# One list for the z units and gate pairs of an encoder layer, and a later place for gate/up's evictions and down sums

## The chip, the core and the metric

The kernel runs on one core of one Trainium2 chip. The metric is the device time of one execution in microseconds (us). It uses five engines: TensorE (PE, with its weight loads as PEld), VectorE (DVE), ScalarE (ACT), GpSimd (POOL) and SyncE (SP, which here issues the DMAs).

## The reference, cut to what matters

One layer of a bidirectional encoder is computed over 1024 tokens and 16 meta tokens, with a model width of 1024, in float32:

```python
h = rmsnorm(h_res, norm1_w[l])
proj = h @ w_in[l]
(q, k, v, z, b_raw, a_raw, sc_b, sc_c, sc_x, gate_a, gate_b) = jnp.split(proj, SPLIT_POINTS, axis=-1)
o_dn = gated_deltanet_bidir(q, k, v, z, b_raw, a_raw, dn_conv_w[l], A_log[l], dt_bias[l], dn_norm_w[l])
y_a = o_dn @ w_branch_dn[l]
y_b = (sc_b * depthwise_conv_centred(sc_c * sc_x, sc_conv_w[l])) @ w_branch_sc[l]
merged = jax.nn.sigmoid(gate_a) * y_a + jax.nn.sigmoid(gate_b) * y_b
h_res = h_res + merged @ w_out[l]
h2 = rmsnorm(h_res, norm2_w[l])
gu = h2 @ w_gate_up[l]
h_res = h_res + (jax.nn.silu(gu[..., :D_FF]) * gu[..., D_FF:]) @ w_down[l]
```

The change touches two stages: the columns z, gate_a and gate_b of the first projection (in `gated_deltanet_bidir` z is used through silu(z)), and `gu` with silu(gate) * up.

## The kernel before, in words

**Numbers as pairs.** Every float32 operand of a product is split in a high part, which ACT casts (`split`, L101), and a low part, which DVE subtracts (L102, `sub` is L179). A product term then takes three matmuls: weight high by data high, weight high by data low, weight low by data high. The matmuls treated here multiply a 128x128 block of weights with 512 tokens.

**The first stage ("z/pair section").** After the scans of the first half of the heads come four *z units*, heads 4 to 7: for each, 128 columns of w_in are loaded, split, and multiplied with the two token halves (24 matmuls each, `dense`, L134 to L136). ACT takes the tanh of half the bank (L1505), DVE makes z*(1+tanh) of it (L1507), SP stores it (L1508). Then come five *gate pairs*, n = 0 to 4 for column blocks j = 3 to 7: gate A's and gate B's block of 128 columns by the two token halves. A pair is done by a scheme of seven products in place of eight: P1 = A11·B11, P2 = A12·B21, S2·T2, S1·T1, S3·T3, S4·B22 and A22·T4 ("TT"), 12 matmuls each (`product`, L1443). Here S1 to S4 are sums of weight blocks ("b1" to "b4": `sums`, L1417 to L1420, with their splits in `stationary2`), T1 to T4 sums of token blocks (`moving_sums`, each formed by DVE in passes 2048 or 1024 elements wide, its high part cast by ACT in one pass of 2048, L1460, its low part subtracted by DVE). T1 to T4 are formed once and serve all pairs. Partial results share a PSUM bank: S2·T2 is added onto P1 in its bank, S3·T3 onto that. So ACT must have copied the bank out before the next product is added: c1 (L1574, into o1's left half) before S2·T2, c2 (L1584) and c3 (L1586) before S3·T3 and S4·B22. DVE adds the other partial results (L1409), ACT takes tanh (`half_turn`, L1511), SP stores both gates (L1597, L1598).

The order of the section up to pair 1 is the order of the code on DVE, PE and ACT: it stands under a manual schedule (`border0`), in which generators (`z_rows`, `pair`, `moving_sums`) are advanced step by step. Pairs 2 to 4 follow outside it, where a scheduler may move instructions. SP's and POOL's queues are ordered by the scheduler throughout. Tiles come from pools: a new tile in the place of an old one waits until the old one's readers are done. The tile that the first token sums are written to (tag `mA`) lies where the stage before had its own tiles.

**Gate/up.** From about 1367 us, 22 columns j of w_gate_up go through the same seven products, 84 matmuls a column. `part1` does P1 and P2 of a column with the copy of the bank, and, unless postponed, the add and Silu (L1765, L1768). Columns 0, 1 and 2 do their `part1` ahead of the loop; the add and Silu of 1 and 2 (`late_evictions`) are called inside column 0. Within a column: the block weights (`block22`, `sums`, `stationary2`), S2·T2, copy u2 (L1847), S1·T1, copy u3 (L1849), S3·T3, add, S4·B22, add, Silu (L1862), multiply, TT, multiply (L1410), stores of the product to DRAM (L1868, L1869). DVE stands under a manual schedule from before column 0 until `border.close()`. `down_sums(k)` loads two blocks of w_down (L1777, L1778), forms four sums on DVE (`sums<-sums`, L179) and stores them (t_d, L1781); it is called for k = j-3 in column j. The sums are read in the last stage only.

Of the kernel before, what the change touches and what calls it, by code (L numbers as in the profile page):

```python
# [8 lines left out]
F32 = mybir.dt.float32  # L9
# [7 lines left out]
P = 128  # L17
# [31 lines left out]
def encoder_layer(ctx: ExitStack, tc: tile.TileContext, x, meta, norm1_w, w_in, w_ba,  # L49
# [1395 lines left out]
    def moving_sums():  # L1445
# [14 lines left out]
        high = lambda n, t: nc.scalar.copy(mov[n][0], t)  # L1460
# [30 lines left out]
        yield
# [5 lines left out]
    z_units = [wload(w_in, unit(OZ + ZH * P))]  # L1497

    def z_rows(h):

        sz = s4(SEQ)
        for sl in (left, right):
            po = psz()
            dense(po, z_units[h - ZH], hx, C0 + META + sl.start, 512)
            nc.scalar.activation(sz[:, sl], po, AF.Tanh, scale=0.5)  # L1505
            yield
            nc.vector.scalar_tensor_tensor(out=sz[:, sl], in0=sz[:, sl], scalar=1.0, in1=po, op0=ALU.add, op1=ALU.mult)  # L1507
        nc.sync.dma_start(z_d[h], sz)  # L1508
        yield
# [3 lines left out]
    def pair_weights(n, j):  # L1513

        s_hl[n % 2] = big(("mB", "mA")[n % 2], [P, 2, 2, KT, P])
        if n == 0:
# [20 lines left out]
        return A_, first, block_sums, second

    def pair(n, j, A_, first, block_sums, second):

        last = j == KT - 1
        o1, o2 = outs[n] = s4(), s4()
        bank = pss()
        if last:
# [474 lines left out]
```

## Time and profile before

| what | value |
|---|---|
| median of the runs shown | 2000.35 us (2000.34, 2000.35, 2001.31) |
| the profiled execution's own time | 2001.08 us |
| its span (first to last instruction) | 1999.33 us, so 1.75 us lie around it |
| granted TensorE clock, mean | 0.998 |
| PE busy | 1972.3 us, 11999 matmuls |
| DVE, ACT, POOL busy | 1396.7, 838.6, 107.0 us |
| z/pair section | 934.95 to 1064 us |
| gate/up, columns 0 to 10 | 1367 to 1580 us |

In the rows of the trace the first number is the start in us, the second the length, then engine, line, operation, the tile written and the tiles read, shapes, a count (several instructions of a kind in a row are one line), and in brackets how long the engine had been idle and what released it. In the rows by stretches the columns are: stretch and its length, busy time and count of PE, PEld, DVE, ACT and POOL, the granted PE clock, the busy share of the DMA engines, GB/s.

### The profile page before, as it was taken

To read this page: it belongs to the slowest core of one execution; us is meant where nothing else is said; L and a number is where in the kernel's file an instruction comes from. 1 tells how busy PE (TensorE), PEld (TensorE's weight loads), DVE (VectorE), ACT (ScalarE), POOL (GpSimd) and SP (SyncE) were. 2 spreads that over 40 slices of the span, in tenths; PEclk is the share of its full clock that TensorE was granted. 3 is DMA by queue.
4 is the path that set the end of the run, shared out by engine and by line. 5 is a ranking of instruction groups with operands and counts; after the bars stand their busy time and mean duration, and the time that the engine had idled before them with its cause. 6 is when DMAs were issued, how large, how long until landed. Compare 5 with 4: busy or idle time off the path is not lost.

```text
span 1999.3 us, 31850 instructions
## 1 busy us (share of the span) xinstructions
PE 1972.3 (99%) x11999; PEld 1718.4 (86%) x11999; DVE 1396.7 (70%) x3015; ACT 838.6 (42%) x1967; POOL 107.0 (5%) x407
## 2 busy tenths in 40 slices
PE   9999999999999999999899999999999999999998
PEld 8999999999999999888778888887878888888887
DVE  6888688888888888846845544468766666656575
ACT  6472354646464646343334221225333333334344
POOL 2011101010101010100000000000000000000000
PEclk9999999999999999999999999999999999999999
DMA  3122222222122212223236743123665345487654
GB/s 133 66 90 74 59 86 59 75 59 75 59 75 59 86 58 65 74 82 104 84 123 236 253 156 96 64 88 124 246 218 209 135 149 188 158 274 243 194 169 173
DMA packets 124546, 251.00 MB, mean 126 GB/s; under 512 B 44966, under 2 KB 46423, under 8 KB 121960
## 3 DMA queue, kind: packets, MB, share of 16 engines
q1 hardware_dynamic: 123815, 247.92, 37.3%
q8 instruction: 94, 1.54, 0.3%
q10 hardware_dynamic: 576, 1.05, 0.1%
q14 instruction: 61, 0.49, 0.1%
HBM read 180.67 MB, written 68.25 MB: 125 GB/s over the span
## 4 chain that ended last, share of the span: by engine, by line
PE 84%; DVE 8%; DMA 4%; ACT 3%; issue 1%; SPq 0%; DVEq 0%; ACTq 0%
PE pm L341 31%; PE pd L1443 10%; PE pe L1443 4%; PE pm L1443 3%; DMA sums<-in_w_down_dram 2%; PE pd L903 1%; PE pd L882 1%; PE pd L866 1%; PE pd L869 1%; PE pe L1927 1%; PE pe L1925 1%; PE pe L1926 1%; PE pd L899 1%; PE pe L603 1%; PE pd L1927 1%
## 5 line engine op out<-in xcount | busy, mean ns | idle before, releaser
L341 PE MATMUL pm<-hTh,wh 128*128 128x320 f32 (+4 forms) x1248 | 428.0, 348 | 0.4 <-ACT hTh L1103 0.2
L341 PE MATMUL pm<-al,wh 128*128 128x320 f32 (+4 forms) x1248 | 427.3, 348 | 0.0
L341 PE MATMUL pm<-hTh,wl 128*128 128x320 f32 (+4 forms) x1248 | 425.6, 346 | 0.0
L341 PEld LDWEIGHTS pm<-hTh,wh 128*128 128x128 f32 x1248 | 233.7, 188 | 12.0 <-issue 1.3
L341 PEld LDWEIGHTS pm<-hTh,wl 128*128 128x128 f32 x1248 | 234.0, 188 | 10.2 <-issue 0.4
L341 PEld LDWEIGHTS pm<-al,wh 128*128 128x128 f32 x1248 | 233.9, 188 | 9.7
L102 DVE TENSOR_TENSOR al<-raw,ring_h 128x1024 fp32r<-128x1024 f32 x73 | 88.6, 1222 | 64.9 <-ACT ring_h L101 64.1
L101 ACT CAST ring_h<-raw 128x1024 fp32r<-128x1024 f32 x73 | 76.7, 1054 | 106.9 <-PE pe L1927 35.0
L363 DVE SCALAR_TENSOR_TENSOR kq<-ra,wc,kq 128x520 f32<-128x520 f32 x128 | 96.5, 754 | 4.9 <-ACT kq L393 4.0
L990 DVE TENSOR_TENSOR wl<-raw,wh 128x512 fp32r<-128x512 f32 x112 | 75.9, 688 | 31.0 <-ACT wh L993 30.4
L889 ACT ACTIVATE w<-pd,small 128x128 f32<-128x128 f32 x128 | 39.8, 363 | 125.0 <-PE pd L882 124.5
L101 ACT CAST wh<-raw 128x1024 fp32r<-128x1024 f32 x49 | 51.4, 1048 | 70.6 <-PE pm L135 17.7
L500 DVE TENSOR_TENSOR fP<-fP,tm 128x135 f32<-128x135 f32 (+23 forms) x248 | 71.7, 289 | 5.1
L496 DVE TENSOR_TENSOR tm<-fP,fN 128x135 f32<-128x135 f32 (+23 forms) x248 | 71.5, 289 | 4.4
L102 DVE TENSOR_TENSOR wl<-raw,wh 128x1024 fp32r<-128x1024 f32 x49 | 59.7, 1219 | 19.4 <-ACT wh L101 19.3
L993 ACT CAST wh<-raw 128x512 fp32r<-128x512 f32 x112 | 66.2, 621 | 3.7 <-issue 3.6
L1862 ACT ACTIVATE b<-b 128x512 f32<-128x512 f32 x22 | 13.9, 631 | 116.2 <-DVE b L1409 116.2
L1409 DVE TENSOR_TENSOR b<-pd,b 128x512 f32<-128x512 f32 x22 | 15.2, 690 | 64.4 <-PE pd L1443 64.4
L1443 PE MATMUL pd<-b,mB 128*128 128x512 f32 x204 | 52.0, 403 | 5.7 <-ACT s L1574 4.9
L1443 PE MATMUL pd<-b_hl,wh 128*128 128x512 f32 x176 | 54.4, 390 | 0.0
L1443 PEld LDWEIGHTS pd<-b,mB 128*128 128x128 f32 x204 | 39.5, 195 | 15.5 <-ACT s L1574 5.3
L856 ACT ACTIVATE jk<-NP 128x128 f32<-128x128 f32 x64 | 19.9, 311 | 76.4 <-DVE NP L852 75.4
(589 smaller groups left out, 4741.9 us busy)
## 6 DMA issues: line engine op xcount, KB each, us to landing
raw<-in_w_in_dram SPq DMA_DIRECT2D x72, 512.0 KB
raw<-in_w_gate_up_dram SPq DMA_DIRECT2D x44, 512.0 KB
sums<-in_w_down_dram SPq DMA_DIRECT2D x22, 512.0 KB
t_d<-sums SPq DMA_DIRECT2D x11, 1024.0 KB
raw<-s_d SPq DMA_DIRECT2D x44, 256.0 KB
raw<-t_d SPq DMA_DIRECT2D x44, 256.0 KB
act_d<-b SPq DMA_DIRECT2D x43, 256.0 KB
raw<-act_d SPq DMA_DIRECT2D x33, 256.0 KB
```

The lines of the kernel that those rows point to most:

```text
L101: nc.scalar.copy(hi, src)
L102: nc.vector.tensor_tensor(out=lo, in0=src, in1=hi.bitcast(F32), op=ALU.subtract)
L341: mm(po[:, :n], ww[:, k], f(k)[:, t0:t0 + n], start=i == 0, stop=i == 3 * KT - 1)
L363: nc.vector.scalar_tensor_tensor(out=acc, in0=raw[:, h0 + t:h0 + t + hn], scalar=wc[:, t, col:col + 1], in1=acc, op0=ALU.mult, op1=ALU.add)
L496: nc.vector.tensor_tensor(out=tv, in0=fP[:, 0:r, j:j + 1].broadcast_to([P, r, n]), in1=fN[:, j:j + 1, j + 1:32].broadcast_to([P, r, n]), o ...
L500: nc.vector.tensor_tensor(out=fP[:, 0:r, j + 1:32], in0=fP[:, 0:r, j + 1:32], in1=tv, op=ALU.subtract)
L603: mm(pk[:, :2 * P].rearrange("p (a t) -> p a t", a=2), kT[:, cs(c)], kq[:, :, cs(c)], start=True, stop=True)
L889: nc.scalar.activation(w[d], b2[:, 2 + d], AF.Copy, scale=ce[:, c, d:d + 1])
L990: nc.vector.tensor_tensor(out=u[1][1][:, k], in0=u[2][:, k], in1=u[1][0][:, k].bitcast(F32), op=ALU.subtract)
L993: nc.scalar.copy(u[1][0][:, k], u[2][:, k])
L1443: mm(po, x[:, k], at(y, k), start=i == 0 and not add_to, stop=i == 11, skip_group_check=add_to)
L1927: mm(bank[t], l_[:, c], h_[:, hi], start=False, stop=last)
```

## The change

In the z/pair section the generators go. Every step (a load's split, a product, a copy, a sum) gets a name, and one list, `SECTION`, names the order in which they are called: T1a to T4c are the passes of the token sums, T1h and T1l a high and low part, z5.0 the products of head 5's first half with its tanh (z5.0t) and finish (z5.0s), g0h, u0h, b01 to b04, sa0h to sb0l the weights of pair 0, P1_0 to TT_0 its products, c, a and h its copies, adds and tanhs. Pairs 2 and 3 follow in the order `PAIR`, S3·T3 now before S4·B22 in all of them. The casts that were L1460, L101 are L1467, L1529, L1538 and L1546 now, the copies c1 to c3 are L1559, tanh L1503 and L1516, the gates' loads L1522 and L1523.

```diff
         f = lambda m: m.bitcast(F32)
@@ -1457,191 +1459,193 @@
         x, y = (big(g, [P, 2, 4, 512], F32) for g in ("mA", "b3"))
         t1, t2, t3, d_ = x[:, 0], x[:, 1], y[:, 0], y[:, 1]
...
-        high = lambda n, t: nc.scalar.copy(mov[n][0], t)
-        low_part = lambda n, t: sub(mov[n][1], t, f(mov[n][0]))
-        sub(t1, h0[1], h0[0])
-        sub(d_, l0[1], l0[0])
-        add(t1, t1, d_)
-        high("T1", t1)
-        yield
...
-        high("T4", t1)
-        yield
-        low_part("T4", t1)
-        yield
+
+        def high(n, t):
+            if n == "T4":
+                m = big("b3", [P, 2, 4, 512])
+                mov[n] = m[:, 0], m[:, 1]
+            nc.scalar.copy(mov[n][0], t)
+        steps.update(T1a=lambda: sub(t1, h0[1], h0[0]), T1b=lambda: sub(d_, l0[1], l0[0]), T1c=lambda: add(t1, t1, d_),
...
+            steps[n + "h"] = lambda n=n, t=t: high(n, t)
+            steps[n + "l"] = lambda n=n, t=t: sub(mov[n][1], t, f(mov[n][0]))
```

```diff
-    outs = {}
-    sums_of_blocks = moving_sums()
-    z0, z1, z2, z3 = (z_rows(h) for h in range(ZH, H))
-    z_units.append(wload(w_in, unit(OZ + (ZH + 1) * P)))
-    next(z0)
-    next(sums_of_blocks)
-    next(sums_of_blocks)
-    next(z0)
-    z_units.append(wload(w_in, unit(OZ + (ZH + 2) * P)))
...
-    pair0 = pair(0, GH, *weights0)
-    weights1 = pair_weights(1, GH + 1)
-    next(pair0)
-    weights1[1]()
-    weights1[2]()
-    for _ in pair0:
-        pass
-    pair1 = pair(1, GH + 1, *weights1)
-    for _ in pair1:
-        pass
```

```diff
+        def sum_high(i):
+            if i == 0:
+                a["s"] = big(("mB", "mA")[n % 2], [P, 2, 2, KT, P])
+            sh, sl = (a["s"][:, m, i] for m in range(2))
+            for x, k in enumerate((("S2", "S4"), ("S3", "S1"))[i]):
+                A_[k] = sh[:, 4 * x:4 * x + 4], sl[:, 4 * x:4 * x + 4]
...
+             "sah": lambda: sum_high(0), "sal": lambda: low_of(a["s"][:, 1, 0], rg, a["s"][:, 0, 0]),
+             "sbh": lambda: sum_high(1), "sbl": lambda: low_of(a["s"][:, 1, 1], ru, a["s"][:, 0, 1]),
+             "P1": lambda: into("bank", "A11", "B11"), "c1": lambda: taken("o1", left, "bank"),
+             "P2": lambda: into("p2", "A12", "B21"), "a1": lambda: added("o1", left, "p2"),
+             "h1": lambda: half_turn(a["o1"][:, left]),
+             "S2": lambda: into("bank", "S2", "T2", True), "c2": lambda: taken("o1", right, "bank"),
+             "S1": lambda: into("bank2", "S1", "T1"), "c3": lambda: taken("o2", right, "bank2"),
+             "S3": lambda: into("bank", "S3", "T3", True), "a3": lambda: added("o2", right, "bank"),
+             "h3": lambda: half_turn(a["o2"][:, right]),
+             "S4": lambda: into("bank2", "S4", "B22", True), "a2": lambda: added("o1", right, "bank2"),
+             "h2": lambda: half_turn(a["o1"][:, right]),
+             "TT": lambda: into("bank", "A22", "T4", True), "h4": last_turn}
+        return d, A_, a, rg, ru, out_tile, stores
...
+    SECTION = """
+        T1a z4.0 z5h T1b z5l T1c z4.1 z4.0t T2a T1h z4.0s T2b T2c z5.0 z4.1t T3a z6h u0h T2h z4.1s z6l u0l
+        b01 z5.1 z5.0t b02 z5.0s T3b T3c T2l z6.0 z5.1t z7h z5.1s T3d z7l T3h T1l z6.1 z6.0t z6.0s T4a T3l
+        z7.0 z6.1t g0h z6.1s u1h g0l b03 b04 T4b sa0h z7.1 z7.0t T4c sb0h z7.0s T4h sa0l sb0l T4l P1_0 z7.1t
+        g1h z7.1s g1l P2_0 c1_0 u1l b11 b12 S2_0 a1_0 b13 h1_0 b14 sa1h S1_0 c2_0 sa1l sb1h sb1l S3_0 c3_0
+        S4_0 a3_0 h3_0 TT_0 a2_0 h2_0 P1_1 h4_0 P2_1 c1_1 S2_1 a1_1 h1_1 S1_1 c2_1 S3_1 c3_1 S4_1 a3_1 h3_1
+        TT_1 a2_1 h2_1 h4_1
+    """
...
+    for k in SECTION.split():
+        steps[k]()
     border0.close()
...
+    for n, j in enumerate(range(GH + 2, KT - 1), 2):
+        d = pair_steps(n, j)[0]
+        for k in PAIR.split():
+            d[k]()
```

In gate/up the block weights of column 1 are written within column 0, and those of column 2 within column 1; `late_evictions` moves from before S4·B22 to behind TT of column 0; DVE's manual schedule ends a column later; the down sums are called for k = j-6 in place of j-3.

```diff
@@ -1826,15 +1830,18 @@
     late_evictions = [p[-1] for p in ahead[1:]]
     split(*mov["T3"], m32[3])
     u_hl[0] = big("w2", [P, 2, 4, P])
+
+    def block_weights(j, rg, ru, A_):
+        block22(j, ru, A_)
+        sums(rg, ru, rg[:, 0:4], rg[:, 4:8], ru[:, 0:4], ru[:, 4:8])
+        stationary2(j, ru, rg, ru, A_)
+
     for j in range(NF):
+        rg, ru, A_, p1, sg, bank, _ = ahead.pop(0) if ahead else part1(stationary1(j), sm[:, j % 2], sm[:, 2 + j % 2])
         if j == 1:
-            s_hl[1] = ap_.tile([P, 2, 2, KT, P], F32R, tag="al0", name="s_hl1")
-            u_hl[1] = ap_.tile([P, 2, 4, P], F32R, tag="al2", name="u_hl1")
-        rg, ru, A_, p1, sg, bank, _ = ahead.pop(0) if ahead else part1(stationary1(j), sm[:, j % 2], sm[:, 2 + j % 2])
-        if j:
-            block22(j, ru, A_)
-            sums(rg, ru, rg[:, 0:4], rg[:, 4:8], ru[:, 0:4], ru[:, 4:8])
-            stationary2(j, ru, rg, ru, A_)
+            block_weights(2, *ahead[0][:3])
+        elif j > 2:
+            block_weights(j, rg, ru, A_)
         u2, u3, r2 = sm[:, 4 + j % 2], sm[:, 6], sm[:, 7]
         if j >= HK:
             k = j - HK
@@ -1855,8 +1862,9 @@
         add(u3, bank, u3)
         if j == 0:
             split(*mov["T4"], m32[2])
-            for f in late_evictions:
-                f()
+            s_hl[1] = ap_.tile([P, 2, 2, KT, P], F32R, tag="al0", name="s_hl1")
+            u_hl[1] = ap_.tile([P, 2, 4, P], F32R, tag="al2", name="u_hl1")
+            block_weights(1, *ahead[0][:3])
         product(bank2, A_["S4"], "B22", True)
         add(u2, bank2, u2)
         nc.scalar.activation(u2, u2, AF.Silu)
@@ -1864,11 +1872,14 @@
         product(bank, A_["A22"], "T4", True, lows_last=j == 0)
         mul(sg, bank, sg)
         if j == 0:
+            for f in late_evictions:
+                f()
+        elif j == 1:
             border.close()
         nc.sync.dma_start(act_d[j][:, 0:512], sg)
         nc.sync.dma_start(act_d[j][:, 512:1024], r2)
-        if 3 <= j <= HK + 2:
-            down_sums(j - 3)
+        if 6 <= j <= HK + 5:
+            down_sums(j - 6)
         if j >= HK:
 
             s1, s4_ = p1, u2
```

What this does to the queues is shown at three places. First DVE, at the start of the z/pair section: `rb` is the last tile of the stage before, `mA` and `b` the tiles of the token sums, `wl` a weight's low part; in brackets what an instruction waits for (DMAHW are DMA queues). Before:

```order
L478 SCALAR_TENSOR_TENSOR rb_12122<-rb_12122,pm_12072 128x512 [waits DMAHW5_49,Activation_49]
L179 TENSOR_TENSOR mA_12177<-hTh 128x2048
L179 TENSOR_TENSOR b_2076_12178<-al_124 128x2048
L1409 TENSOR_TENSOR mA_12177<-mA_12177,b_2076_12178 128x2048 [waits DVE_49]
L179 TENSOR_TENSOR mA_12177<-hTh,mA_12177 128x2048 [waits DVE_49]
L1409 TENSOR_TENSOR mA_12177<-mA_12177,al_125 128x1024 [waits DVE_49]
```

And after the change:

```order
L478 SCALAR_TENSOR_TENSOR rb_12122<-rb_12122,pm_12072 128x512 [waits DMAHW5_49,Activation_49]
L179 TENSOR_TENSOR mA_12138<-hTh 128x2048 [waits DMAHW1_49,DMAHW4_49,DMAHW0_49,DVE_49]
L179 TENSOR_TENSOR b_2068_12139<-al_124 128x2048
L179 TENSOR_TENSOR wl_12187<-raw_12142,wh_12186 128x1024 [waits DMAHW6_49,PE_49]
L1409 TENSOR_TENSOR mA_12138<-mA_12138,b_2068_12139 128x2048 [waits DVE_49]
L179 TENSOR_TENSOR mA_12138<-hTh,mA_12138 128x2048 [waits DVE_49]
L1507 SCALAR_TENSOR_TENSOR s_2083_12217<-s_2083_12217,pe_12161 128x512 [waits Activation_49]
```

The first pass on `mA` waits for three DMA queues now, before for none; the low part `wl` and a finish of a z unit stand among the passes.

Second ACT, around the copies of pair 0 (`s<-pd` are c1 and c2, `wh`, `u_hl` and `mB` or `mA` the high parts of weights). Before:

```order
L101 CAST mB_12318<-raw_12323 128x1024
L1460 CAST b_2098_12396<-mA_12177 128x2048
L1505 ACTIVATE s_2096_12359<-pe_12401 128x512
L1574 COPY s_2107_12439<-pd_12441 128x512
L1511 ACTIVATE s_2107_12439<-s_2107_12439 128x512
L101 CAST wh_12433<-raw_12435 128x1024
L101 CAST u_hl_12431<-raw_12436 128x512
L101 CAST wh_12655<-raw_12657 128x1024
L1584 COPY s_2107_12439<-pd_12441 128x512
```

And after the change:

```order
L1467 CAST b_2103_12429<-mA_12138 128x2048
L1503 ACTIVATE s_2102_12424<-pe_12399 128x512
L1529 CAST wh_12448<-raw_12152 128x1024
L1559 COPY s_2108_12467<-pd_12434 128x512
L1529 CAST wh_12658<-raw_12654 128x1024
L1516 ACTIVATE s_2108_12467<-s_2108_12467 128x512
L1546 CAST mA_12488<-raw_12152 128x1024
L1559 COPY s_2108_12467<-pd_12434 128x512
L1546 CAST mA_12488<-raw_12153 128x1024
```

The cast of T4 stands ahead of c1 in both. Pair 1's high part of a block sum (L1546, `mA<-raw`) stands ahead of c2 now, where before two casts of pair 1's plain weights and pair 2's did.

Third DVE in gate/up, from the low part of T4 (`b<-al`, L102) in column 0 on. Before:

```order
L1409 TENSOR_TENSOR b_2363_14871<-pd_14912,b_2363_14871 128x512
L1417 TENSOR_TENSOR raw_14889<-raw_14889 128x512
L1418 TENSOR_TENSOR raw_14889<-raw_14888,raw_14889 128x512
L102 TENSOR_TENSOR b_2384_14993<-al_14128,b_2384_14993 128x2048
L1409 TENSOR_TENSOR b_2363_14871<-pe_14979,b_2363_14871 128x512
L1409 TENSOR_TENSOR t_2391_15004<-pm_15019,t_2390_15003 128x512
L1409 TENSOR_TENSOR b_2363_14871<-pe_15035,b_2363_14871 128x512
L1419 TENSOR_TENSOR raw_14888<-raw_14889,raw_14888 128x512
L102 TENSOR_TENSOR s_hl_15118<-raw_14889,s_hl_15118 128x1024
L1410 TENSOR_TENSOR b_2363_14871<-b_2363_14871 128x512
L1410 TENSOR_TENSOR b_2363_14871<-pd_14912,b_2363_14871 128x512
L1420 TENSOR_TENSOR raw_14888<-raw_14888 128x512
```

And after the change:

```order
L102 TENSOR_TENSOR b_2384_14993<-al_14128,b_2384_14993 128x2048
L102 TENSOR_TENSOR u_hl_15084<-raw_14889,u_hl_15084 128x512
L1417 TENSOR_TENSOR raw_14889<-raw_14889 128x512
L1418 TENSOR_TENSOR raw_14889<-raw_14888,raw_14889 128x512
L1419 TENSOR_TENSOR raw_14888<-raw_14889,raw_14888 128x512
L1420 TENSOR_TENSOR raw_14888<-raw_14888 128x512
L179 TENSOR_TENSOR sums_15748<-sums_15748 128x512
L102 TENSOR_TENSOR s_hl_15083<-raw_14888,s_hl_15083 128x1024
L102 TENSOR_TENSOR s_hl_15083<-raw_14889,s_hl_15083 128x1024
```

Column 1's four block sums and the low part `u_hl` follow T4's low part at once, with one pass of the down sums between; the four adds and two multiplies that stood among them come later.

More of the change, by code (lines that the diff above doesn't have):

```diff
@@ L1443, in product, with moving_steps @@
             mm(po, x[:, k], at(y, k), start=i == 0 and not add_to, stop=i == 11, skip_group_check=add_to)
-    def moving_sums():
+    steps = {}
+    def moving_steps():
         c = [slice(C0 + META + 512 * i, C0 + META + 512 * i + 512) for i in range(2)]
@@ L1644, in encoder_layer, with high, corner @@
-    o1 = outs[KT - 1 - GH][0]
+        g0, g1, u0, u1 = rg[:, 0:4], rg[:, 4:8], ru[:, 0:4], ru[:, 4:8]
+        def high():
+            gh, gl = a["g"] = wtiles([P, KT, P])
+            A_["A11"], A_["A12"] = (gh[:, 0:4], gl[:, 0:4]), (gh[:, 4:8], gl[:, 4:8])
+            nc.scalar.copy(gh, rg)
+        def corner():
+            if n == 0:
+                u = big("w2", [P, 2, 4, P])
+                u_hl[0] = u[:, 0], u[:, 1]
+            elif n == 1:
+                u_hl[1] = [tp.tile([P, 4, P], F32R, tag="t2", name=uid("u_hl"), bufs=2) for _ in range(2)]
+            A_["A22"] = u_hl[n % 2]
+            nc.scalar.copy(u_hl[n % 2][0], u1)
```

232 lines of the change are left out of this document (100 added, 132 removed).

## The prediction

> **What bounds the kernel now.** I read the page's busy times first, then the 40 slices, then stretches where PE falls short, and there the waits and the timeline.
>
> ```profile
> PE 1972.3 (99%) x11999; PEld 1718.4 (86%) x11999; DVE 1396.7 (70%) x3015; ACT 838.6 (42%) x1967; POOL 107.0 (5%) x407
> 950.00:1000.00 50.00, 44.46 (x186) 35.98 (x185) 39.96 (x37) 18.61 (x23) 0.00 (x0) 0.93 0.24 84
> 1350.00:1400.00 50.00, 46.07 (x210) 36.66 (x208) 44.05 (x58) 26.45 (x32) 0.00 (x0) 1.00 0.36 125
> PE pd L1443 <- ACT s L1574: 4.9, 1, 4.9
> ```
>
> PE bounds: all its idle time is 1999.3 − 1972.3 = 27 us, and the change touches no matmul, so it can only win or lose idle time and clock. PE lacks most in the stretches shown: 5.5 us at 950–1000 (z/pair section) and 3.9 us at 1350–1400 (column 0 of gate/up). The waits name the largest stop, 4.9 us on c1 (L1574).
>
> ```profile
> 934.95:1064.00 129.05, 122.53 (x524) 98.76 (x523) 84.50 (x82) 49.55 (x65) 0.00 (x0) 0.97 0.32 113
> 934.95:983.94 48.99, 48.99 (x217) 40.35 (x215) 42.08 (x33) 16.36 (x19) 0.00 (x0) 1.00 0.30 104
> 983.94:988.96 5.02, 0.16 (x1) 0.00 (x0) 3.60 (x4) 2.87 (x3) 0.00 (x0) 0.75 0.54 193
> 988.96:993.80 4.84, 4.84 (x12) 3.84 (x13) 3.21 (x4) 2.31 (x4) 0.00 (x0) 0.55 0.27 108
> 980.99 0.39 PE L1443 MATMUL pd<-hTh,wl 128*128 128x512 f32 x1
> 993.81 2.88 PE L1443 MATMUL pm<-b,mB 128*128 128x512 f32 x12
> 997.37 0.50 PE L1443 MATMUL pm<-hTh,mB 128*128 128x512 f32 x1 [0.68 <-ACT s L1586]
> 997.71 0.39 PE L1443 MATMUL pm<-al,mB 128*128 128x512 f32 x1
> 1003.95 3.01 PE L1443 MATMUL pd<-b,w 128*128 128x512 f32 x12 [0.84 <-DVE s L1409]
> 986.04 1.90 ACT L1460 CAST b<-mA 128x2048 fp32r<-128x2048 f32 x1 [3.81 <-DVE mA L1409]
> 988.33 0.58 ACT L1574 COPY s<-pd 128x512 f32<-128x512 f32 x1
> ```
>
> The pace is 216 matmuls (eight z products of 24, P1 and P2) in 49.0 us, 0.227 each. Then PE stands for 5.0 us: c1 is a short copy of a bank whose last matmul came at 980.99, but it stands on ACT behind T4's cast, which waited 3.81 us for DVE's last pass on `mA`. Behind the stop 12 matmuls take 4.84 us in place of 12·0.227 = 2.72, at a granted clock of 0.55: 2.1 us more. Two later stops of 0.68 and 0.84 us cost some 0.27 each beyond their idle time: the matmul after 997.37 starts 0.34 behind it (0.11 too much), and the twelve ahead, from 993.81, were over at 996.5, 0.16 before the idle time begins. **Loss of the section:** 5.0 + 2.1 + 0.68 + 0.84 + 2·0.27 = 9.2 us, which agrees with the whole stretch: 129.05 less 528·0.2268 (four of its matmuls have no record) is 9.3.
>
> **The change in the z/pair section.** Nothing is computed more or less; DVE, ACT and SP get the same passes in another order. In the new list c1 no longer waits: T4's cast and c1 stand behind DVE passes that come earlier, since the weights of pair 0 and the finishes lie among them where DVE had to wait before. To see what is late next I add up DVE's queue to pair 1's last block sum (b14), for the list puts c2 on ACT behind the cast of that sum (sa1h).
>
> ```profile
> 935.90 0.60 ACT L474 ACTIVATE rb<-pm 128x512 f32<-128x512 f32 x1
> 936.04 1.23 DVE L102 TENSOR_TENSOR wl<-raw,wh 128x1024 fp32r<-128x1024 f32 x1 [3.40 <-ACT wh L101]
> 937.18 0.68 DVE L478 SCALAR_TENSOR_TENSOR rb<-rb,pm 128x512 f32<-128x512 f32 x1
> 937.78 2.28 DVE L179 TENSOR_TENSOR mA<-hTh 128x2048 f32<-128x2048 f32 x1
> 939.98 2.28 DVE L179 TENSOR_TENSOR b<-al 128x2048 f32<-128x2048 f32 x1
> 956.06 0.68 DVE L1507 SCALAR_TENSOR_TENSOR s<-s,pm 128x512 f32<-128x512 f32 x1
> 956.66 0.68 DVE L1507 SCALAR_TENSOR_TENSOR s<-s,pe 128x512 f32<-128x512 f32 x1
> 977.28 0.69 DVE L1417 TENSOR_TENSOR raw<-raw 128x512 f32<-128x512 f32 x1
> 978.00 0.69 DVE L1418 TENSOR_TENSOR raw<-raw,raw 128x512 f32<-128x512 f32 x1
> 992.03 1.03 ACT L101 CAST wh<-raw 128x1024 fp32r<-128x1024 f32 x1
> 932.46 0.33 SPq L480 DMA_DIRECT2D z_d<-rb  x1
> 933.50:934.00 0.50, 0.50 (x6) 0.43 (x5) 0.00 (x0) 0.20 (x1) 0.00 (x0) 1.00 0.96 361
> 934.00:934.50 0.50, 0.50 (x6) 0.46 (x4) 0.00 (x0) 0.42 (x2) 0.00 (x0) 1.00 0.03 8
> ```
>
> From start to start a DVE pass of 2048 takes 2.20, of 1024 1.14, of 512 0.60 us, and 0.12 more when it reads what the pass before it wrote (0.72 at 977.28).
>
> - *The new wait.* The first pass, T1a, waits for DMA queues now; by the tiles I take it to be the store of the last `rb`. L478, which fills `rb`, is free once ACT is through with it at 936.5, ends at 937.2, and its store goes out at 937.3. The equal store of 932.46 had left the DMA engines by 934.4 (share 0.96, then 0.03): 2.0 us. So T1a starts at 939.3, not 937.8. Queued behind it is everything that DVE does in the section.
> - *The sum.* Down to b14 the queue holds 11 passes of 2048, 14 of 1024 (one is pair 2's low part, which the scheduler put in) and 19 of 512, seven of them dependent: 24.2 + 16.0 + 11.4 + 0.8 = 52.4 us. No pass among them waits longer than its forerunner's end by these durations, so b14 ends at 991.7.
> - *What is late.* sa1h (1.03) ends at 992.8, c2 (0.58) at 993.3. PE has done 240 matmuls (S2·T2 and S1·T1 more) by 934.95 + 240·0.227 = 989.4, with 0.2 for the last one's drain. So it **stands for 3.7 us ahead of S3·T3**. This takes the place of the 5.0 us on c1. The other passes keep 0.5 us or more before their products.
> - *The clock.* The stop is shorter than the 5.0 us that cost 2.1. Bounds are nothing and 2.1: the stop of 2.34 us at 1387.55 (its row is below) left the clock at 1.00 in 1350–1400, the one of 5.0 halved it. 3.7 lies between the two; I take 1.3.
> - SP issues the same loads and stores; the gates' loads lie beside the z products (24 matmuls, 5.4 us each). Without that cover a load of 512 KB would show with 1.4 us at the 376 GB/s of the last row below.
>
> Sum: 9.2 goes; 3.7 + 0.27 + 1.3 = 5.3 comes. **The section wins 3.9 us.**
>
> [...]
>
> ```profile
> 984.00:988.00 4.00, 0.10 (x1) 0.00 (x0) 2.58 (x4) 1.96 (x2) 0.00 (x0) 0.81 0.67 242
> 988.00:992.00 4.00, 3.04 (x7) 2.46 (x8) 3.46 (x3) 1.42 (x3) 0.00 (x0) 0.50 0.08 32
> 992.00:996.00 4.00, 4.00 (x16) 3.21 (x16) 2.91 (x4) 3.01 (x5) 0.00 (x0) 0.84 0.25 99
> ```
>
> With 0.81 granted over 984–988 the clock fell 2.5 us after PE's last matmul, and with 0.84 over 992–996 it came back some 4.3 us after the restart. [...]
>
> **The change in gate/up.** The first stops come from column 0 and 1, the later from down sums.
>
> ```profile
> 1381.70 2.11 PE L1443 MATMUL pd<-b,w 128*128 128x512 f32 x8 [0.48 <-ACT b L101]
> 1387.55 2.56 PE L1443 MATMUL pm<-s,s_hl 128*128 128x512 f32 x10 [2.34 <-DVE s_hl L102]
> 1390.44 0.73 PE L1443 MATMUL pd<-mA,s_hl 128*128 128x512 f32 x2 [0.32 <-ACT s_hl L101]
> 1400.28 1.89 PE L1443 MATMUL pd<-b,u_hl 128*128 128x512 f32 x7 [1.01 <-DVE b L1409]
> 1381.68 2.29 DVE L102 TENSOR_TENSOR b<-al,b 128x2048 fp32r<-128x2048 f32 x1
> 1489.35 2.15 DVE L179 TENSOR_TENSOR sums<-sums 128x512 f32<-128x512 f32 x3 [4.63 <-DMA sums<-in_w_down_dram]
> 1492.15 2.14 PE L1443 MATMUL pd<-b,w 128*128 128x512 f32 x8 [1.80 <-DVE b L1409]
> 1564.41 2.79 PE L1443 MATMUL pd<-b,mB 128*128 128x512 f32 x11 [0.70 <-ACT b L1847]
> ```
>
> - *Columns 0 and 1.* In the new order T4's low part (2.20 from 1381.2, half a microsecond earlier, as `u_hl` stands behind it now) is followed by `u_hl` (0.60) and four dependent sums (0.72 each): 1386.9, the cast (1.05) 1388.0, and the second low part 2·1.14 later, 1390.4. PE, which waits for these same weights, stands about 0.1, 0.5, 2.2, 1.0 and 1.1 us, 4.9 with what surrounds each, against 5.2 so measured in before (0.48, 2.34, 0.32 and 1.01, 0.27 more each). Gain 0.3. The postponed evictions hold banks that PE needs only in column 1: cover of some 5 us.
> - *Later.* The stop at 1492.15 is a DVE that waited 4.63 us for a load of w_down and held the add behind it. The calls move three columns, but SP's order shifts these loads by one product group only; the second load still stands behind two loads of weights. I expect the same pattern at the neighbouring columns: 1.9 at one and 0.7 at another, in place of 1.80 and 0.70, and one more of 0.3.
> - *Net:* 0. Below it could reach −4.3 (all later stops gone: 1.80 + 0.70 + 2·0.27 = 3.0, and the 1.01 + 0.27 at 1400.28), above +4.1 (two more of 1.80 with their restarts).
>
> **Sum.** 2001.08 − 3.9 + 0 = **1997.2 us**. The profiled execution is 0.7 above the median; its 2.1 us of half clock may be less in other executions, and as I put 1.3 in its place the sum needs no second correction.
>
> **Rivals.**
>
> - *R1, no stop is left.* DVE is early enough, or c2 gets ahead of the cast: 2001.08 − 9.2 = 1991.9. It needs b14 3.7 us earlier; dropping the new wait gives 1.5 and pair 2's low part 1.1. The profile speaks against it: DVE is busy 42.1 of 49.0 us in the section.
> - *R2, the stop stays but the clock does not fall,* as behind the 2.34 us: 1997.2 − 1.3 = 1995.9. That it fell after 2.5 us in 984–988 speaks against it. [...]
> - *R3, the new wait is longer.* The store of `rb` shares the DMA engines with the 512 KB loads issued behind it.
>
> ```profile
> 940.00:944.00 4.00, 4.00 (x19) 3.34 (x18) 3.96 (x3) 0.60 (x1) 0.00 (x0) 1.00 0.94 376
> ```
>
> At 376 GB/s 1.25 MB take 3.5 us; with 1.0 from issue to transfer (932.46 to 933.5) the store would land 4.5 us after issue, 2.5 later: 1999.7.
>
> - *R4, slower.* DVE's passes for the down sums wait for loads ahead of adds that PE needs, in more columns than before. One such wait cost 1.80 us. Five more: 1997.2 + 9.0 = 2006.2. It turns slower beyond 2004.35 from the fourth one on (2004.4).
> - That the change doesn't do what it says is out for the section, where the queues are as listed; for the down sums it is in the forecast.
>
> **How the numbers follow.** About 0.2% (4.0 us) can be told from no change here: 1996.35 and 2004.35. Chances: the forecast 0.61, of its own range 1994.8 to 1999.3; R1 0.07; R2 0.14; R3 0.10; R4 0.08. Faster: R1, most of R2 (0.10) and 0.21 of the forecast, 0.38. Slower: R4, 0.08. Same: 0.54. The range takes in R2, R3 and the forecast with most of gate/up's bounds (−3.9, +3.2): 1993.3 to 2000.4; R1, R4 and the tails are left out.
>
> **What would show it.** In the new profile: T1a on DVE starts near 939.3 behind a DMA; c1 is no longer a releaser of PE; PE stands once, near 989.5 for 3 to 4 us, released by ACT's copy L1559, which stands behind L1546; the next 4 us have a granted clock under 0.9; pair 3 ends its products about 4 us earlier than 1064. In gate/up PE stands 2 us near 1386 on `s_hl`, nothing at 1400, and DVE still waits 4 to 5 us for w_down once or twice. The forecast is wrong if DVE has gaps before b14, or if c2 does not end last there.

## The result, and the profile after

The changed kernel takes 1998.16 us (median of 12 runs, 1994.81 to 2000.32), the kernel before 1999.92 us (12 runs, 1998.33 to 2004.04). The ratio is 0.9989 with a 95% interval of 0.9981 to 0.9997: some 2 us faster, between 0.6 and 3.8, which is less than the 4 us that the prediction gives as the least that can be told from no change. The profiled execution took 1998.42 us, with a span of 1996.67. Two of the eleven runs of E5 below took 3281.99 and 4908.73 us; its figures are those of the other nine.

First the two stages that the change touches, as stretches from their first to their last matmul, before and after. (The section starts at 934.95 us in the one and 935.83 in the other; between the two stages both traces take 267.5 us, behind gate/up 217.4 and 217.5.)

```profile
934.95:1084.40 149.45, 142.94 (x613) 115.27 (x612) 94.73 (x93) 62.15 (x81) 0.00 (x0) 0.98 0.38 134
1351.90:1781.90 430.00, 423.11 (x1866) 347.87 (x1865) 293.31 (x396) 156.90 (x212) 0.00 (x0) 1.00 0.53 183
```

```profile
935.83:1080.84 145.01, 140.97 (x613) 115.55 (x612) 93.81 (x93) 62.27 (x81) 0.00 (x0) 0.99 0.40 138
1348.38:1779.20 430.82, 425.32 (x1867) 350.29 (x1866) 293.87 (x396) 157.47 (x212) 0.00 (x0) 0.99 0.52 183
```

The section is 4.4 us shorter with the same 613 matmuls, gate/up 0.8 us longer, although PE is idle there for 5.5 us in place of 6.9: its busy time rose by 2.2 us at a lower clock.

In the section, DVE's start and its pass for pair 1's last block sum, ACT's queue around pair 0's copies, and PE, in the changed kernel:

```profile
937.41 0.69 DVE L478 SCALAR_TENSOR_TENSOR rb<-rb,pm 128x512 f32<-128x512 f32 x1 [3.91 <-ACT rb L474]
940.64 2.29 DVE L179 TENSOR_TENSOR mA<-hTh 128x2048 f32<-128x2048 f32 x1 [2.54 <-DMA z_d<-rb]
992.42 0.69 DVE L179 TENSOR_TENSOR raw<-raw 128x512 f32<-128x512 f32 x1
```

```profile
984.75 0.58 ACT L1559 COPY s<-pd 128x512 f32<-128x512 f32 x1
993.19 1.04 ACT L1546 CAST mA<-raw 128x1024 fp32r<-128x1024 f32 x1 [0.74 <-DVE raw L179]
994.14 0.58 ACT L1559 COPY s<-pd 128x512 f32<-128x512 f32 x1
```

```profile
985.38 3.04 PE L1443 MATMUL pd<-b,mB 128*128 128x512 f32 x12 [0.41 <-ACT s L1559]
988.26 2.88 PE L1443 MATMUL pm<-b,mB 128*128 128x512 f32 x12
994.77 4.37 PE L1443 MATMUL pd<-b,mB 128*128 128x512 f32 x12 [3.63 <-ACT s L1559]
996.00:1000.00 4.00, 4.00 (x12) 3.11 (x11) 1.61 (x2) 0.20 (x2) 0.00 (x0) 0.57 0.76 222
```

T1a waits 2.54 us for the store of `rb`. c1 (the copy of 984.75) is early and leaves 0.41 us of the 4.87. c2 (994.14) stands behind the cast of pair 1's block sum, which waited for DVE; PE stands 3.63 us for it, and the clock falls to 0.57 behind the stop.

In gate/up, PE in columns 0 and 1 and at the late stop, with DVE ahead of each:

```profile
1383.16 0.73 PE L1443 MATMUL pm<-s,s_hl 128*128 128x512 f32 x2 [1.99 <-ACT s_hl L101]
1384.56 0.73 PE L1443 MATMUL pd<-mA,s_hl 128*128 128x512 f32 x2 [0.66 <-ACT s_hl L101]
1385.82 4.63 PE L1443 MATMUL pd<-mA,s_hl 128*128 128x512 f32 x10 [0.53 <-DVE s_hl L102]
1386.00:1390.00 4.00, 4.00 (x10) 3.14 (x11) 3.96 (x7) 0.63 (x1) 0.00 (x0) 0.50 0.65 222
1509.94 1.45 PE L1443 MATMUL pd<-b,u_hl 128*128 128x512 f32 x5 [2.14 <-DVE b L1409]
```

```profile
1377.63 2.29 DVE L102 TENSOR_TENSOR b<-al,b 128x2048 fp32r<-128x2048 f32 x1 [1.38 <-ACT b L101]
1380.56 0.69 DVE L1417 TENSOR_TENSOR raw<-raw 128x512 f32<-128x512 f32 x1
1507.14 2.15 DVE L179 TENSOR_TENSOR sums<-sums 128x512 f32<-128x512 f32 x3 [4.71 <-DMA sums<-in_w_down_dram]
```

The stop at 1400 is gone. In its place stand three stops on `s_hl` close together, and 4 us at half clock behind them. T4's low part waits 1.38 us for ACT's cast, and column 1's sums start only behind it; in the kernel before, two of them ran in that time (1380.22 to 1381.62, the low part at 1381.68).

### The profile page after: what moved, and what is told of

Read it like the earlier page. It is cut to its first block, busy times and chain, and to the rows that moved or that the text cites. A ratio compares the mean times of both kernels' runs of the same rounds, so it can differ in the third digit from the quotient of the medians.

```text
span 1996.7 us, 31849 instructions
## 1 busy us (share of the span) xinstructions
PE 1972.5 (99%) x11999; PEld 1720.9 (86%) x11999; DVE 1397.0 (70%) x3015; ACT 840.4 (42%) x1967; POOL 106.7 (5%) x407
## 4 chain that ended last, share of the span: by engine, by line
PE 85%; DVE 9%; ACT 2%; DMA 2%; issue 1%; SPq 0%; DVEq 0%; ACTq 0%
PE pm L341 28%; PE pd L1443 12%; PE pe L1443 5%; PE pm L1443 4%; PE pd L882 1%; PE pd L903 1%; PE pd L866 1%; PE pe L1938 1%; PE pe L1937 1%; PE pe L1936 1%; PE pd L869 1%; PE pd L899 1%; PE pe L603 1%; PE pd L1938 1%; PE pd L1937 1%
## 5 line engine op out<-in xcount | busy, mean ns | idle before, releaser
L341 PE MATMUL pm<-al,wh 128*128 128x320 f32 (+4 forms) x1248 | 427.3, 348 | 0.0
L102 DVE TENSOR_TENSOR al<-raw,ring_h 128x1024 fp32r<-128x1024 f32 x73 | 88.6, 1222 | 64.9 <-ACT ring_h L101 64.3
L101 ACT CAST ring_h<-raw 128x1024 fp32r<-128x1024 f32 x73 | 76.7, 1053 | 106.9 <-PE pd L1938 38.3
L101 ACT CAST wh<-raw 128x1024 fp32r<-128x1024 f32 x40 | 42.0, 1050 | 70.2 <-PE pm L135 18.5
L1409 DVE TENSOR_TENSOR b<-pd,b 128x512 f32<-128x512 f32 x22 | 15.2, 690 | 64.0 <-PE pd L1443 64.0
L102 DVE TENSOR_TENSOR wl<-raw,wh 128x1024 fp32r<-128x1024 f32 x40 | 48.8, 1219 | 7.1 <-ACT wh L101 7.0
L876 DVE SCALAR_TENSOR_TENSOR r<-pd,negEG,vS 128x128 f32<-128x128 f32 x120 | 36.7, 344 | 20.8 <-PE pd L866 20.6
```

Of the source, the lines that this page charges most:

```text
L101: nc.scalar.copy(hi, src)
L102: nc.vector.tensor_tensor(out=lo, in0=src, in1=hi.bitcast(F32), op=ALU.subtract)
L341: mm(po[:, :n], ww[:, k], f(k)[:, t0:t0 + n], start=i == 0, stop=i == 3 * KT - 1)
```

## The experiments

Each was timed beside the kernel before on one chip. E1 to E4, E5 to E8, E9 to E11 and E12 ran on four different chips, so across these groups the ratios are compared and not the medians. Medians and ratios first:

| kernel | median us (runs) | ratio to before, 95% | section | gate/up |
|---|---|---|---|---|
| changed kernel | 1998.16 (12) | 0.9989 (0.9981–0.9997) | 145.0 | 430.8 |
| E1 section only | 1995.48 (11) | 0.9981 (0.9972–0.9990) | 146.2 | 428.4 |
| E2 gate/up only | 2001.98 (11) | 1.0010 (1.0001–1.0019) | 149.3 | 430.6 |
| E3 changed, c2 and c3 early | 1994.07 (7) | 0.9969 (0.9958–0.9980) | 140.5 | 432.4 |
| E4 changed, wait covered | 1995.58 (11) | 0.9983 (0.9974–0.9992) | 142.8 | 429.9 |
| E5 down sums only | 1999.14 (9) | 1.0001 (0.9991–1.0010) | 149.0 | 429.3 |
| E6 weights and evictions only | 2001.43 (11) | 1.0015 (1.0007–1.0024) | 150.0 | 428.7 |
| E7 changed, E3 and E4 | 1991.58 (5) | 0.9963 (0.9950–0.9977) | 138.8 | 430.3 |
| E8 as E7, gate/up of before | 1988.94 (5) | 0.9951 (0.9938–0.9963) | 138.8 | 427.9 |
| E9 as E8, evictions late | 1989.97 (5) | 0.9949 (0.9936–0.9963) | 138.8 | 429.1 |
| E10 as E8, weights early | 1993.45 (5) | 0.9966 (0.9954–0.9979) | 138.8 | 432.9 |
| E11 as E9, sums in the hole | 1988.35 (5) | 0.9940 (0.9928–0.9953) | 138.8 | 427.3 |
| E12 as E11, w_down by POOL | 1998.06 (11) | 0.9984 (0.9975–0.9993) | 138.8 | 441.4 |

The last two columns are the lengths of the two stages in the one profiled execution of each, first to last matmul, in us (before: 149.4 and 430.0). The gate/up of before alone measured 427.9 to 430.0 in four traces (before, E1, E5, E8): a single trace tells a stage to about 1 us.

### E1 and E2: which half of the change

E1 is the kernel before with the list, E2 the kernel before with the four edits of gate/up.

```diff
 E1, against before
-    sums_of_blocks = moving_sums()
...
+    for k in SECTION.split():
+        steps[k]()
 E2, against before
+            block_weights(1, *ahead[0][:3])
...
+            for f in late_evictions:
+                f()
...
+            down_sums(j - 6)
```

> Only the z/pair section is changed, gate/up is as before. My theory: the section carries the whole gain. The stop of 4.9 us on c1 is gone, one of 3.4 to 3.9 us ahead of S3·T3 has come (released by c2 behind the cast of pair 1's block sum), behind it half clock for 0 to 2 us: 3 to 5 us less than before, ratio to before 0.9975 to 0.9985. In gate/up the stops of before are there (2.3 on s_hl near 1387, 1.8 near 1492). Rival: the gain comes from gate/up and the section is even: ratio 0.9995 to 1.0005.

> Only gate/up is changed, the z/pair section is as before. My theory: even, between 2 us less and 1 us more (idle time some 2 us less, as the stop at 1400 goes and one near 1510 takes the place of those at 1492 and 1564; the half clock behind the three stops of column 0 costs 0 to 3): ratio 0.999 to 1.0005, and the 4.9 us stop on c1 is there. Rival: gate/up carries the gain, ratio 0.9985 or less.

E1 is faster than before by 0.1% to 0.28%, E2 slower by 0.01% to 0.19%. The two medians against before (−4.0 and +2.5 us) add up to −1.4, near the −1.8 of the whole change. So the section carries the gain, and gate/up loses half of it again. My expectation for E2, even, was wrong at its upper end.

### E3, E4 and E7: what holds the section

E3 puts pair 0's copies ahead of the cast in ACT's queue, E4 exchanges the first two passes, E7 does both, all on the changed kernel.

```diff
-P2_0 c1_0 u1l b11 b12 S2_0 a1_0 b13 h1_0 b14 sa1h S1_0 c2_0 sa1l sb1h sb1l S3_0 c3_0
+P2_0 c1_0 u1l b11 b12 S2_0 a1_0 b13 c2_0 S1_0 c3_0 h1_0 b14 sa1h sa1l sb1h sb1l S3_0
-T1a z4.0 z5h T1b z5l T1c
+T1b z4.0 z5h T1a z5l T1c
```

> The changed kernel, with pair 0's copies c2 and c3 called ahead of the cast of pair 1's block sum, so that they stand ahead of it on ACT; nothing else moves. My theory: S3·T3 waits for c2 alone, and c2 only for its place in ACT's queue, so the stop of 3.6 us goes and the half clock behind it: no stop over 0.3 us from 985.5 to 1060 beyond the 0.4 ahead of S2·T2, 3.8 to 5.3 us less than the changed kernel, ratio to before 0.996 to 0.9972. Rival: DVE is the limit (it starts 2.5 us late behind the new wait), and the stop comes back at the next product that needs pair 1's weights (S2·T2 of pair 1) with 2 us or more: ratio to before 0.998 to 0.999.

> The changed kernel, with the first two passes of the token sums exchanged: the one on the low parts (it waits for no DMA) runs while the tile mA still waits for the store of rb. My theory: DVE gets 2.2 of its 2.5 us back, the last block sum of pair 1 is 2.2 us earlier, the stop ahead of S3·T3 shrinks from 3.6 to 1.4 us and leaves the clock at full: 2.2 to 3.6 us less than the changed kernel, ratio to before 0.997 to 0.998; the 0.4 us stop ahead of S2·T2 goes too. Rival: other waits on DVE (for ACT's casts, for loads) take up the 2.2 us, and the stop stays over 3 us.

> The changed kernel with both edits of the section: c2 and c3 ahead of the cast, and the first two passes exchanged. My theory: the stops that were left in the section (0.4 ahead of S2·T2, 0.7 ahead of TT on an add that came late) go with the 2.2 us that DVE gains: 0.5 to 1.8 us less than with the copies alone, some 5 less than the changed kernel, ratio to before 0.996 to 0.997. Rival: the copies alone had taken everything, and the ratio is theirs, 0.9969.

E3's section has two stops left, the 0.41 us on c1 and one ahead of pair 0's last product:

```profile
997.55 3.04 PE L1443 MATMUL pd<-b,w 128*128 128x512 f32 x12 [0.73 <-DVE s L1409]
936.05:1076.60 140.55, 139.41 (x613) 114.41 (x612) 93.54 (x93) 62.42 (x81) 0.00 (x0) 1.00 0.41 143
```

The 3.63 us and the half clock are gone, at 1.00 throughout. The queue order was the cause; DVE was the limit only through it. E4's T1a still starts at 940.24, but the other pass is done by then, and its stop is 2.18 us (I expected 1.4: as PE loses no 0.68 us ahead of S2·T2 any more, it comes to S3·T3 earlier). Even so the clock falls:

```profile
992.17 4.14 PE L1443 MATMUL pd<-b,mB 128*128 128x512 f32 x10 [2.18 <-ACT s L1559]
993.00:996.00 3.00, 3.00 (x9) 2.33 (x8) 1.22 (x1) 0.56 (x2) 0.00 (x0) 0.50 0.57 187
```

With both edits PE has no idle time in the section and the clock is full; the section is 1.7 us shorter than E3's, and by the ratios the kernel is 1.2 us faster, within the 0.5 to 1.8 that I had put on the last stops (their intervals overlap, so the times alone don't show it):

```profile
935.73:1074.55 138.82, 138.82 (x613) 114.53 (x612) 93.71 (x93) 62.23 (x81) 0.00 (x0) 1.00 0.41 145
```

### E5, E6, E8, E9 and E10: what gate/up loses

E5 is the kernel before with the down sums' line alone, E6 is E2 without it. E8 has the list with both edits of E7 and gate/up as before, and serves as the base for E9 (evictions behind TT) and E10 (weights a column earlier, evictions and down sums where they were).

```diff
 E5, against before
-        if 3 <= j <= HK + 2:
-            down_sums(j - 3)
+        if 6 <= j <= HK + 5:
+            down_sums(j - 6)
 E9, against E8
             split(*mov["T4"], m32[2])
-            for f in late_evictions:
-                f()
...
         if j == 0:
+            for f in late_evictions:
+                f()
             border.close()
```

> The kernel before, with the down sums alone called three columns later. Theory A (the loss of gate/up lies in columns 0 and 1: three stops that together are longer, with half clock behind them): even with before, ratio 0.9996 to 1.0004, with the stops of 2.3 us near 1387 and 1 us near 1400 as before. Theory B (the loss lies in the down sums, whose loads hold DVE ahead of an add near 1510): ratio 1.0005 to 1.0015, one stop of 2 to 2.6 us on an add near 1510, or two.

> The kernel before, with gate/up's block weights a column earlier and the evictions later, but the down sums where they were. Theory A: it has the whole loss of gate/up, ratio 1.0005 to 1.0015, with stops of 2.0, 0.7 and 0.5 us on s_hl between 1383 and 1390 and half clock behind them. Theory B: even or a little faster, ratio 0.9992 to 1.0002 (the stop at 1400 is gone), since the late stop stays at 1492.

> The list of the section with both edits, gate/up as before. My theory: what the section wins and what gate/up loses add up, so this is 1.5 to 3 us faster than the same section with the changed gate/up: 1990 to 1992.5, ratio to before 0.9952 to 0.9965. Rival: gate/up's loss depends on how the two halves of the kernel meet, and this one is no faster than the same with the changed gate/up.

> The section with both edits and gate/up as before, but for the evictions of columns 1 and 2, which stand behind TT of column 0. The queue of DVE then has one add in place of three ahead of the low part that PE waits for in column 1. My theory: this part of the change is a gain, 1.2 us off the stop of 2.3 us on s_hl, which leaves the clock at full more often: 1986 to 1988.5, ratio to before 0.9935 to 0.9947. Rival: PE waits next on a bank that the evictions hold, and the time is that of the same kernel without the edit, 1989, or more.

> The section with both edits, gate/up with the block weights a column earlier, but the evictions and the down sums where they were before. My theory: the early weights are the loss. The code calls column 1's four sums behind T4's low part, which waits 1.5 us for ACT, while before two of them ran in that hole; so the casts and low parts come later: stops on s_hl of 3.5 to 5 us together between 1370 and 1385, half clock behind, 1991 to 1994, ratio to before 0.996 to 0.9975. Rival: the loss was the late evictions: 1988 to 1990, as with gate/up of before.

E5 is even with before, E6 has the loss. So it lies in the weights and evictions of columns 0 to 2. (E6's one trace doesn't show it: its gate/up is 428.7 us long, though its runs reach from 1998.56 to 2005.50.) E5's edit moves little, though: its loads of w_down go out from 1384.1 to 1543.8 us, those of the kernel before from 1384.0 to 1544.5, as the scheduler orders SP's queue. So E5 says that this edit costs nothing, and not what later down sums would cost. E8 is faster than E7 by 2.6 us in the medians, as the sum of the parts says, though one of E7's five runs was as fast (1988.19). E10, with the early weights and the old evictions, is the slowest of E8 to E11: 3.5 us above E9 on the same chip, where the runs of the two don't overlap (1991.02 to 1994.50, 1988.90 to 1990.18), and by the ratios 3 us above E8. Its PE in columns 0 and 1, and the DVE pass that explains it:

```profile
1377.96 1.22 PE L1443 MATMUL pm<-s,s_hl 128*128 128x512 f32 x2 [3.18 <-ACT s_hl L101]
1380.54 1.22 PE L1443 MATMUL pd<-mA,s_hl 128*128 128x512 f32 x2 [1.35 <-ACT s_hl L101]
```

```profile
1371.23 2.29 DVE L102 TENSOR_TENSOR b<-al,b 128x2048 fp32r<-128x2048 f32 x1 [1.38 <-ACT b L101]
1373.44 0.68 DVE L1409 TENSOR_TENSOR b<-pe,b 128x512 f32<-128x512 f32 x1
1374.04 0.68 DVE L1409 TENSOR_TENSOR t<-pm,t 128x512 f32<-128x512 f32 x1
1375.36 0.69 DVE L1417 TENSOR_TENSOR raw<-raw 128x512 f32<-128x512 f32 x1
```

DVE waits 1.38 us with nothing, then come T4's low part and two evictions, then the first sum. In the change the evictions are out of the way, and the stops are shorter (1.99, 0.66 and 0.53 us in place of 3.18 and 1.35); the ratios of E7 and E10, 0.9963 and 0.9966, don't tell whether that makes it faster. Alone the late evictions gain nothing that the ratios show (E9 0.9949, E8 0.9951), against my expectation of 1.2 us. The first stop did shrink from 2.34 to 1.15 us, but the two adds and the two multiplies now stand ahead of the fourth sum, the second half of the weights is late, and half clock follows that second stop:

```profile
1376.32 2.56 PE L1443 MATMUL pm<-s,s_hl 128*128 128x512 f32 x10 [1.15 <-DVE s_hl L102]
1381.02 0.73 PE L1443 MATMUL pd<-mA,s_hl 128*128 128x512 f32 x2 [2.14 <-ACT s_hl L101]
1383.00:1385.00 2.00, 2.00 (x6) 1.55 (x5) 2.00 (x3) 0.92 (x1) 0.00 (x0) 0.50 0.81 240
```

### E11: the order that follows

E11 is E9 with column 1's weights written out by halves: `u_hl` and two sums ahead of T4's low part, then that half's low part, then the rest.

```diff
-            split(*mov["T4"], m32[2])
+            split(u_high, u_low, u1)
+            tt(out=u1, in0=u0, in1=u1, op=ALU.add)
+            tt(out=u0, in0=g0, in1=u0, op=ALU.subtract)
+            split(*mov["T4"], m32[2])
+            split(*halves[1], ru)
+            tt(out=g0, in0=u1, in1=g0, op=ALU.subtract)
+            tt(out=g1, in0=g1, in1=g0, op=ALU.subtract)
+            split(*halves[0], rg)
```

> As the kernel with the evictions late, and column 1's weights in an order that follows from the theory: u_hl and the first two sums ahead of T4's low part, in the time in which DVE waits for ACT, then the low part of these two, then the other two sums. Column 2 is as before. My theory: the stops on s_hl shrink to under 1 us each, with the clock at full: 1985.5 to 1987.5, ratio to before 0.993 to 0.9942. Rival: PE waits for ACT's casts in any case, and the stops stay near 2 us: 1988 to 1990.

```profile
1378.52 0.73 PE L1443 MATMUL pd<-mA,s_hl 128*128 128x512 f32 x2 [0.61 <-ACT s_hl L101]
1379.80 2.56 PE L1443 MATMUL pd<-mA,s_hl 128*128 128x512 f32 x10 [0.55 <-DVE s_hl L102]
```

The stop of 2 us is gone. Four short ones remain in columns 0 and 1 (0.32, 0.61, 0.55 and 0.21 us), and the clock stays full there. The runs are 1986.90 to 1988.42 us, E9's 1988.90 to 1990.18 on the same chip, so 1.6 us came out of it by the medians. The late stop was longer in E11's trace than in E9's (2.51 us at 1500, 1.35 at 1482), which takes back a part. E11 is the fastest version tried, faster than both kernels, by 0.47% to 0.72% against before.

### E12: a queue of their own for w_down

The late stop came in most traces at one column or another (1.80 us at 1492 before, 2.14 at 1510 after). SP's queue in E11 ahead of its late stop, and DVE's wait:

```profile
1486.73 0.33 SPq L1781 DMA_DIRECT2D sums<-in_w_down_dram  x1
1488.85 0.33 SPq L1759 DMA_DIRECT2D raw<-in_w_gate_up_dram  x1
1490.12 0.33 SPq L1758 DMA_DIRECT2D raw<-in_w_gate_up_dram  x1
1490.50 0.42 SPq L1782 DMA_DIRECT2D sums<-in_w_down_dram  x1
```

```profile
1497.33 2.15 DVE L179 TENSOR_TENSOR sums<-sums 128x512 f32<-128x512 f32 x3 [4.91 <-DMA sums<-in_w_down_dram]
```

The second load of w_down is issued 3.8 us behind the first, after two loads of gate/up weights. E12 issues both from POOL.

```diff
-        nc.sync.dma_start(r[:, 0], w_down[k * P:k * P + P, :])
+        nc.gpsimd.dma_start(r[:, 0], w_down[k * P:k * P + P, :])
```

> As the kernel with the sums in the hole, but the two loads of w_down for each down sum are issued by POOL, which does nothing else then, in place of SP. My theory: the late stop of 2.5 us near 1500 comes from SP's order (the second load of w_down is issued 3.7 us behind the first, behind two loads of gate/up weights, and DVE holds an add behind it); with a queue of their own both loads go out together, DVE's waits of 4 to 5 us for w_down go, and the late stop shrinks to under 0.5 us: 1985 to 1987, ratio to before 0.9925 to 0.9938. Rival: the loads are late because the DMA engines are full there (0.6 of their time), so DVE waits as before and the time is the same, 1988.

```profile
1418.82 0.53 POOL L1781 DMA_DIRECT2D sums<-in_w_down_dram  x1 [16.13 <-DMA t_d<-sums]
1419.34 0.53 POOL L1782 DMA_DIRECT2D sums<-in_w_down_dram  x1
1422.00:1424.00 2.00, 2.00 (x11) 1.65 (x10) 0.00 (x0) 0.00 (x0) 0.00 (x0) 1.00 0.87 330
1426.40 0.69 DVE L179 TENSOR_TENSOR sums<-sums 128x512 f32<-128x512 f32 x1 [6.01 <-DMA sums<-in_w_down_dram]
1429.26 1.07 PE L1443 MATMUL pd<-b,u_hl 128*128 128x512 f32 x2 [4.21 <-DVE b L1409]
```

My theory fell: by the ratios 9 us were lost against E11, and DVE's waits for w_down in gate/up came to 31.0 us (11 waits) in place of 17.3 (8). The loads go out together, but beside two of gate/up weights and one of act_d, issued between 1417.55 and 1419.34; the DMA engines are busy (0.87 over 1422–1424), and the first load is there 7.6 us after its issue. DVE waits 6 us in place of 5, and the add that PE waits for (L1409, at 1428.52) stands behind two passes of the sums. Nor did the other queue let the loads go earlier: POOL stood 16.13 us until the store of the sums before them (`t_d<-sums`) was through with the tile that the loads write, and in E11 SP's queue waits for that store too (21.6 us in 8 waits from 1400 to 1600). A second tile for the sums wasn't tried, nor DVE without these passes ahead of its adds; and whether POOL's queue is itself slower than SP's is open.

## Why the prediction was right, and where it was off

Forecast were 1997.2 us, measured 1998.16. That they lie 1 us apart is in part luck. The sum started from one execution of 2001.08 us, 1.2 us above the median of twelve runs, 1999.92; from that median 3.9 us less would be 1996.0. The 2 us that gate/up lost were not in the sum, and the two errors point opposite ways. By the prediction's own steps:

- **The stop on c1 goes, one of 3.7 us on c2 comes.** Shown: 3.63 us, released by L1559 behind L1546. E3 proves the cause, as the stop goes with the place in the queue. The size is helped by two shifts that cancel: c2 ended 58.9 us into the section and not 58.35, and PE was through with its 240 matmuls at 55.3 and not 54.65.
- **The new wait.** Right in kind; the store took 2.5 us and not 2.0, so T1a starts 4.8 us into the section and not 4.35. That pushed DVE's queue, and c1 with it, so that 0.41 us remained on c1 where I had said none. DVE's 44 passes then ran without a gap, as summed: from 940.64 to the last sum's end at 993.1 are 52.5 us against 52.4.
- **The clock.** 1.3 us taken between 0 and 2.1. In the trace 7 matmuls of 0.43 us in place of 0.227, 1.4 us, stand by themselves. In E1's trace, behind the same stop (3.60 us), PE's busy time in the section is 1.2 us longer still, so there the clock took some 2.6 us by this estimate, more than my upper bound. Neither trace shows R1, no stop, or R2, the full clock.
- **The section.** 3.9 us less forecast; 4.4 in the pair of traces, 3.2 in E1's trace, 4.0 by E1's median.
- **Gate/up: the term that was mis-sized.** I put net 0. It is +2 us (E2: 1.0001 to 1.0019). The stops were where I put them, the early ones shorter (0.5, 2.2, 1.0 and 1.1 us forecast, 0.19, 1.99, 0.66 and 0.53 found), the late one of 1.9 at 2.14. What I left out is the clock: the three stops close to each other ended in half clock, 0.50 over 1386–1390 where before 1388–1392 was at 1.00. I had costed the clock behind the section's stop only. And I did not see that the 1.4 us in which DVE waits for ACT had been filled before. But one pair of traces overstates the clock: with gate/up as before it fell behind the 2.34 us stop in E1, E5 and E8, and only the trace of the kernel before kept it. The kernel before, then E1:

```profile
1388.00:1392.00 4.00, 3.62 (x15) 2.29 (x14) 4.00 (x7) 1.53 (x2) 0.00 (x0) 1.00 0.83 298
1388.00:1391.00 3.00, 3.00 (x10) 2.03 (x9) 3.00 (x6) 1.11 (x2) 0.00 (x0) 0.61 0.62 234
```

Over the four traces with gate/up as before PE is idle for 5.2 us and busy for 423.7 in the mean, over five with the changed one (the changed kernel, E2, E3, E4, E7) 5.8 and 425.0. So of 1.9 us some 1.3 are a slower PE and 0.6 idle time, an estimate, as traces of one kind differ by more than that.

- **R3 and R4.** The store was not held up for 4.5 us (R3), and DVE did not wait more for w_down (R4): 12.5 us in 11 waits, before 16.8 in 10. E5, which is even, is no test of R4, as its loads go out when they did before.

So a net gain of 2 us is a gain of 4 and a loss of 2, and the larger part of what the list could give (10.6 us in the section, by E7's trace) was held back by one copy's place in ACT's queue and one pass's place in DVE's.

## What to carry to other kernels

When an order is written out by hand, read each queue for short releases behind long work: here a copy of 0.58 us behind a cast that waited for DVE left PE standing for 3.63 us, and moving it was worth about as much as the rest of the list (4.5 us of the section in E3's trace, 4.4 from before to the changed kernel). A list also fixes the holes: what a scheduler had put into a wait is not put there again unless the list names it. And price a stop together with the clock behind it, by the stops that stand near each other and not each alone: in the changed kernel 1.99, 0.66 and 0.53 us close together ended at 0.50 for 4 us, the 2.14 us that stood alone at 1.00.

## What the runs showed of the hardware

- **Half clock after short stops.** Of the single stops between 2.1 and 2.6 us in these traces, half were followed by half clock (2.18 in E4, 2.34 in E1, E5 and E8, 2.45 in E3, 2.42 in E12) and half were not (2.34 before, 2.14 in the changed kernel, 2.20 in E4, 2.54 in E2, 2.60 in E7, 2.51 in E11); of those from 1.0 to 1.8 that stood alone none was (1.00 behind 1.01 and 1.80 before), of those over 3 all were (0.55 behind 4.87 before, 0.57 behind 3.63 in the changed kernel). E9's 2.14, 4.7 us behind the start of the product that follows its stop of 1.15, ended in half clock too (0.50 over 1383–1385). The clock granted behind the single ones was 0.50 over 993–996 in E4 and 0.61 over 1388–1391 in E1, and 1.00 over 1388–1392 in the kernel before, 1510–1514 in the changed kernel, 1503–1506 in E7 and 1500–1504 in E11. The same 2.34 us were followed by half clock in three traces and not in a fourth, and in E4 2.18 us were and 2.20 were not: the length of a single stop of this size does not tell it, and what does was not shown.
- **The kernels differed in their scatter.** Among those with five runs, E8, E9 and E11 reach over 1.3 to 1.6 us, E10 over 3.5 and E7 over 5.4; E6, with eleven, over 6.9 (1998.6 to 2005.5). The wide ones have the early weights and their stops close together. That the clock makes the scatter is not shown: in E6 the two fastest runs were granted 0.998 and the four slowest 0.994 to 0.996, but a run of 2001.43 had 0.998 too, and E8's trace has half clock behind a stop of 2.34 us.
- **A load beside four others was late.** In E12 a load of 512 KB was there 7.6 us after its issue when five loads were issued within 1.8 us; the median of E12's 22 loads of w_down was 5.8 us, the quickest took 3.7.
